# One decoder step on one core: merge statistics in one group, gate rows early, another order of delta heads, five early gate tiles

## The chip, the cores and the metric

The kernel runs on one core of a Trainium2 chip. The metric is the device time of one execution in microseconds (us); three runs of the kernel before took 942.03, 938.55 and 942.79 us, median 942.03 us. Engines are named as the profile names them: PE is TensorE (matmul), PEld its weight load, DVE is VectorE, ACT is ScalarE, POOL is GpSimd, SP is SyncE, which issues nearly all DMAs here and does no arithmetic.

## The reference

One layer of a hybrid decoder, in float32, for one prompt of 512 tokens and 8 samples of 4 new tokens each (544 token columns), model width 1024. Cut to what matters:

```python
shift, scale, gate = split(silu(c) @ w_cond + b_cond, 3)
h = x * (1 + scale) + shift
qa, ka, va, za, qkv_b, zb, a_b, b_b, ga, gb = split_columns(h @ w_in)       # 11280 columns
# branch A: 3 groups of 8 heads, windows 128/512/2048 with dilation 1/4/16
for g in range(3): out[g], lse[g] = dilated_attend(qa[g], ka[g], va[g], bias[g])
o_a = einsum('g..., g...d -> ...d', softmax(lse over g), out)               # the merge
ya = o_a * silu(za)
# branch B: 8 delta heads: causal conv (width 4) + silu, l2norm, chunked delta rule
state, o_b = gated_delta(state0, q, k, v, g, beta)
yb = rmsnorm(o_b) * b_norm_w * silu(zb)
merged = sigmoid(ga) * (ya @ w_branch_a) + sigmoid(gb) * (yb @ w_branch_b)
y = layernorm(ALPHA * x + gate * (merged @ w_out)) * ln_g + ln_b
```

The samples also read caches of keys and values and states of the delta rule; caches and states are outputs too.

## The kernel before, in words

**The stream.** The projection `h @ w_in` is cut into 88 column tiles of 128 columns. One tile is one job: its weight is loaded by SP (512 KB), split into a high and a low part (`hi` by ACT, `lo` by DVE), and multiplied in 2 halves of 272 token columns, 8 pieces of the contraction and 3 products each, so 48 matmuls of 128x272 (`pp<-hhi,hi`, `pp<-hlo,hi`, `pp<-hhi,lo`). A half lies in one of two PSUM banks (`pp`) until ACT and DVE have read it out (`evac`); only then can the half after the next begin. Jobs run strictly in the order of the list `jobs`.

**The order before.** With c0 to c7 for the three jobs (k, q, v) of a delta head (`conv_job`) and r0 to r3 for the nine jobs of an attention round (two heads of each of three groups, `attention_job`), the list is c0, r0, c1, c2, r1, c3, c4, r2, c5, c6, six jobs of r3, c7, three jobs of r3, za0, za1, zb0, zb1, za2, za3, zb2 to zb7, then gate and branch jobs.

**Beside the stream** run threads of other work, planned with lower rank numbers (0 first): the delta rule (`delta_rule`, rank 0), its preparation (`delta_blocks`, rank 1), prompt attention (`prompt_attention`, rank 3), attention of the samples over their caches for the first half of the heads (`early`, rank 4); the stream has rank 9. A planner in the kernel (`Recorder.schedule`) lists all instructions with costs and dependences and writes each engine's order; the hardware then runs each engine's list in order, with semaphores. Operations inside `with rec.together():` are held together: once the first is taken, PE takes nothing else until the last.

**Buffers the change touches.** A head's k and q lie in a tile `KQ`, of which there are two. So the first conv of head h+2 (`KQ<-ext,acc` on DVE) can write only after the last matmul of head h's delta rule that reads it (`pd<-S,KQ`). Conv rows `ext` have two buffers as well. Pool `op` (tag `o`) has nine buffers of 128x544 for slabs of early sample attention, later for `zt`, `nd`, `ybh` and `yal`, handed out in the order of first use.

**The merge.** After rounds 1 and 3 the minima and sums of the softmax (`st`) are turned by 40 small matmuls into `pt` (`pg<-cst,st`), DVE and ACT make weights `R`, these go to DRAM and come back broadcast (`dw<-R`, `wv<-dw`), and DVE weighs `ya` and `NB`. The matmuls of one strip of 32 PE columns (one value of r) follow one another, then the next strip's; they are not held together.

**The boundary after round 3.** The jobs zb0 and zb1 are early (`EARLY_B = 2`): their `zt` lies in pool `op` and they are finished later. The `zt` of zb2 to zb7 lies in a pool `zp` that opens only when the pools of attention and delta rule are closed, so after the last merge operation. Behind the boundary lies the samples' chain: `sample_decays` (tile `nd`), `sample_delta`, and sample attention of the second half of the heads (`kv` tiles), whose result is copied into `ya`; the branch jobs of A (`pp<-yah,hi`) need it. Seven gate jobs of A (`EARLY_A = 7`) stand ahead of them.

**The gate rows** (`gate_rows`, rank 1, the last stretch of the stream): `gate` of prompt and samples, `silu(c) @ w_cond[:, 2048:]`, in 16 matmuls with 32 columns of weights (`pd<-wc,cs`), then four selecting matmuls (`pg<-Y,cst`: for each half one that repeats the prompt's row 128 times into `gp` and one that spreads the samples' rows into `gs`), added to the bias.

Of the kernel before, what the change touches and what calls it, by code (L numbers as in the profile page):

```python
# [11 lines left out]
F32 = mybir.dt.float32  # L12
# [23 lines left out]
BANKS = (2, 2, 3, 1)  # L36
MOVE = 128
MOVES = (48.0, 850.0)
EARLY_A, EARLY_B = 7, 2
S0B = 7  # L40


# [201 lines left out]
class Recorder:  # L244
# [20 lines left out]
    def pool(self, make, name, bufs, side):  # L265
        return Pool(self, make, name, bufs, side)
# [456 lines left out]
def body(ctx, tc, io):  # L723
# [71 lines left out]
    def cond_product(part, load, ps):  # L795


        for k, n, wc in load(part):
            q = (k + 2 * n) % 4
            pe.matmul(ps[n][32 * q:32 * q + 32, :], cs[:, k, :], wc, start=(k < 4), stop=(k >= 4),  # L800
                      tile_position=(0, 32 * q))
            yield

    def cond_rows(part, k0, nk):
        return io["w_cond"][k0 * 128:(k0 + nk) * 128, part * D:(part + 1) * D].rearrange("(k p) c -> p k c", p=128)
# [165 lines left out]
    tail = d0.tile([128, 34], F32, name="tail")  # L971
    etot = d0.tile([128, 34], F32, name="etot")
    dO = dram.tile([8, 128, 512], F32, name="dO")
    qd = dram.tile([2, 2, NS, 256], F32, name="qd")
    us = d0.tile([128, 3, 8, NS], F32, name="us")
    oS = keep.tile([128, 8, NS], F32, name="oS")
# [406 lines left out]
    def attention_job(j, g, s):  # L1383

        def begin():
            pairs[j][s, g] = spare()[:, :SEQ] if s == 2 else ap.tile([128, 512], F32, name="qk"[s], bufs=3)

        def evac(n, ps):
            t, scale = pairs[j][s, g], 1.0 if s else -0.125
            if g == 0:  # L1390
                lo, hi = ((0, 272), (272, 512))[n]
                se.activation(t[:, lo:hi], ps[:, 0:hi - lo], AF.Copy, scale=scale)
            else:
                v = t.rearrange("p (r a n) -> p n a r", r=4, a=4)
                m = (17, 15)[n]
                se.activation(v[:, 17 * n:17 * n + m], ps[:, 0:16 * m].rearrange("p (n a r) -> p n a r", a=4, r=4),
                              AF.Copy, scale=scale)
            if n:
                se.activation((qs, ks, vs)[s][:, j, g, :], ps[:, 240:272], AF.Copy, scale=scale)
                if s == 2:  # L1400
                    threads.set(ready[j, g], 2.5)

        return column_job(("a", j, g, s), evac=evac, begin=begin, start=(freed[j - 1] if j else began,))

    def prompt_attention():

        for j in range(4):
# [95 lines left out]

            pt = pg()
            ve.memset(pt, 1.0)
            for kd in range(4):
                for r in range(4):
                    o = pt[32 * r:32 * r + 4, 128 * kd:128 * kd + 128]
                    if kd % 2:
                        pe.matmul(o, st[:, kd, r, :], ident, start=True, stop=True, tile_position=(0, 32 * r))  # L1510
                        continue
                    for i in range(4):
                        pe.matmul(o.rearrange("p (a n) -> p n a", a=4)[:, 8 * i:8 * i + 8, :], st[:, kd, i, :],
                                  ident[:, r:128:4], start=True, stop=True, tile_position=(0, 32 * r))
            R = ap.tile([128, 4, 128], F32, name="R", tag="P", bufs=2)
            Z = ap.tile([128, 4, 128], F32, name="Z", tag="P", bufs=2)
            two = lambda t: t[:, None, :].to_broadcast([128, 2, 128])
# [437 lines left out]

    def gate_rows():

        b = io["b_cond"][:, 2 * D:]
        sp.dma_start(gp, b.to_broadcast([128, D]))
        sp.dma_start(gs, b.to_broadcast([64, D]))  # L1960
        ps = [pd(), pd()]
        yield 4.0
        for n in range(2):
            w = slice(512 * n, 512 * n + 512)

            for k0 in range(0, KT, 4):
                wc = []
                for k in (k0, k0 + 2):
                    wc.append(wcp.tile([128, 2, 512], F32, name="wc"))
                    sp.dma_start(wc[-1], cond_rows(2, k, 2)[:, :, w])  # L1970
                with rec.together():
                    take(cond_product(2, lambda part: ((k0 + k, n, wc[k // 2][:, k % 2]) for k in range(4)), ps), 99)
                yield 2.0
            Y = zp.tile([128, 512], F32, name="Y", tag="rbo")
            se.activation(Y, ps[n], AF.Copy)
            yield 1.8
            for t, r, sel in ((gp, 128, C("selc")[:, 0:1].to_broadcast([128, 128])), (gs, 64, C("selg"))):
                p = pg()
                pe.matmul(p[0:r], sel, Y, start=True, stop=True)
                ve.tensor_add(t[:, w], t[:, w], p[0:r])  # L1980


    for s in (1, 0, 2):
        jobs.append(conv_job(0, s))
    h = 1
    for j in range(4):
        nine = [attention_job(j, g, s) for g in range(3) for s in range(3)]
        if j == 3:
            jobs += nine[:6] + [conv_job(7, s) for s in (1, 0, 2)] + nine[6:]
        else:  # L1990
            jobs += nine + [conv_job(h + i, s) for i in range(2) for s in (1, 0, 2)]
            h += 2
    jobs += [za_job(j) for j in range(2)] + [zb_job(h, True) for h in range(EARLY_B)] + [za_job(j) for j in range(2, 4)]
    jobs += [zb_job(h) for h in range(EARLY_B, 8)]
    mt, yah, yal, mhi, mlo = {}, {}, {}, {}, {}
    mT = mt
    of_b = (lambda k: ybh[k], lambda k: ybl[k])
# [19 lines left out]
    def early():  # L2017
# [4 lines left out]
        yield tuple(ready[3, g] for g in range(3))  # L2022
        sample_queries(1, slabs()[0:64, 0:256], qr1)

    threads.add(early(), 4)

    def prep():
# [62 lines left out]
            se.activation(wo[n][0][:, k:k + 2], raw, AF.Copy)  # L2090
            ve.tensor_sub(wo[n][1][:, k:k + 2], raw, wo[n][0][:, k:k + 2].bitcast(F32))

    wctx = ExitStack()
    wcp = pool(wctx, "wcp", 3, "right")

    def merge_after(m):
        def after():
            t = gate_tile["ga", m]
# [10 lines left out]

    for m in range(8):  # L2110
        jobs += [gate_job("ga", m)] * (m >= EARLY_A) + [branch_job("ga", m, 4, of_a, after=merge_after(m))]
    threads.add(gate_rows(), 1)
    threads.add(stream(len(jobs)), 9)
    threads.run(lambda: not threads.parts)
    wctx.close()
    zctx.close()
    gates_ctx.close()
    octx.close()
# [181 lines left out]
```

## Time and profile before

| | us |
|---|---|
| median of three runs | 942.03 |
| profiled execution | 939.77 |
| its span | 938.0 |
| PE busy | 892.0 |
| DVE busy | 736.8 |
| ACT busy | 417.0 |

The profile is of one execution; 1.8 us of its time lie outside the span. A busy PE is not a PE at its peak, since matmuls overlap: the stream's matmuls start 0.125 us apart while each is recorded as 0.29 us long. A program's matmul in plain float32 appears as two records. In a row of the timeline stand start, duration, engine, line (L670 is the planner's helper, so instructions are told apart by their tiles), operation, out<-in, shape and, in square brackets, how long the engine sat idle before and what ended it. In a row of windows stand the stretch, its length, then busy time and number of instructions of each engine, the granted PE clock, the busy share of the 16 DMA engines and GB/s.

### The profile page before, as it was taken

To read this page: it belongs to the slowest core of one execution; us is meant where nothing else is said; L and a number is where in the kernel's file an instruction comes from. 1 tells how busy PE (TensorE), PEld (TensorE's weight loads), DVE (VectorE), ACT (ScalarE), POOL (GpSimd) and SP (SyncE) were. 2 spreads that over 40 slices of the span, in tenths; PEclk is the share of its full clock that TensorE was granted. 3 is DMA by queue.
4 is the path that set the end of the run, shared out by engine and by line. 5 is a ranking of instruction groups with operands and counts; after the bars stand their busy time and mean duration, and the time that the engine had idled before them with its cause. 6 is when DMAs were issued, how large, how long until landed. Compare 5 with 4: busy or idle time off the path is not lost.

```text
span 938.0 us, 20669 instructions
## 1 busy us (share of the span) xinstructions
PE 892.0 (95%) x8070; PEld 825.8 (88%) x8070; DVE 736.8 (79%) x1620; ACT 417.0 (44%) x975; POOL 64.0 (7%) x176
## 2 busy tenths in 40 slices
PE   4799999999999999999999998988999999999995
PEld 1599999999989999979999997877999999998784
DVE  1575556876799999889989997556899789957768
ACT  0365347753557443576725753441532222234411
POOL 0120000200011110010100200001020000000000
PEclk9799999999999999999999999998999999999998
DMA  9677773658878778786787868459689899988613
GB/s 357 226 220 238 221 246 136 224 182 251 272 249 273 229 250 287 236 292 219 241 301 242 277 206 298 140 172 365 219 267 360 340 418 377 361 284 306 205 43 112
DMA packets 106341, 237.76 MB, mean 253 GB/s; under 512 B 30898, under 2 KB 62140, under 8 KB 103556
## 3 DMA queue, kind: packets, MB, share of 16 engines
q1 hardware_dynamic: 106244, 236.45, 73.8%
q8 instruction: 63, 1.03, 0.4%
q14 instruction: 34, 0.28, 0.1%
HBM read 220.40 MB, written 103.70 MB: 346 GB/s over the span
## 4 chain that ended last, share of the span: by engine, by line
PE 72%; DVE 11%; DMA 4%; ACT 3%; issue 2%; SPq 0%; POOL 0%; DVEq 0%; POOLq 0%; ACTq 0%
PE pp L670 55%; PE pg L670 7%; PE pd L670 6%; PE pb L670 3%; DVE slab L670 2%; DMA dO<-orow 1%; DMA wv<-dw 1%; DMA slab<-in_vs 1%; DVE lo L670 1%; ACT L670 1%; DVE XF L670 1%; DVE r L670 1%; ACT hi L670 1%; DVE ya L670 1%; DVE acc L670 0%
## 5 line engine op out<-in xcount | busy, mean ns | idle before, releaser
L670 PE MATMUL pp<-hhi,hi 128*128 128x272 f32 x1408 | 415.6, 295 | 11.3 <-DVE zt L670 8.7
L670 PE MATMUL pp<-hhi,lo 128*128 128x272 f32 x1408 | 415.3, 295 | 0.0
L670 PE MATMUL pp<-hlo,hi 128*128 128x272 f32 x1408 | 414.1, 294 | 0.2 <-DVE small L670 0.2
L670 PEld LDWEIGHTS pp<-hhi,hi 128*128 128x128 f32 x1408 | 267.2, 190 | 13.7 <-DVE zt L670 9.1
L670 PEld LDWEIGHTS pp<-hlo,hi 128*128 128x128 f32 x1408 | 267.2, 190 | 2.7 <-issue 0.9
L670 PEld LDWEIGHTS pp<-hhi,lo 128*128 128x128 f32 x1408 | 266.5, 189 | 3.3 <-issue 1.8
L670 ACT ACTIVATE hi<-wt 128x1024 fp32r<-128x1024 f32 (+1 forms) x104 | 106.8, 1027 | 167.7 <-PE pp L670 144.8
L670 DVE TENSOR_TENSOR lo<-wt,hi 128x1024 fp32r<-128x1024 f32 (+1 forms) x104 | 122.5, 1178 | 54.8 <-ACT hi L670 54.0
L670 DVE SCALAR_TENSOR_TENSOR acc<-ext,cw,acc 128x568 f32<-128x568 f32 x72 | 57.5, 799 | 0.7
L670 ACT ACT_TABLE_LOAD x38 | 48.8, 1283 | 9.3 <-DMA cT<-in_cT 8.0
L670 DVE TENSOR_TENSOR slab<-slab 128x512 f32<-128x512 f32 (+1 forms) x66 | 42.4, 663 | 3.7 <-DMA slab<-in_vs 3.1
L670 DVE TENSOR_REDUCE slab<-slab 128x8 f32<-128x512 f32 (+2 forms) x66 | 42.4, 655 | 0.3
L670 ACT ACTIVATE P<-P,st 128x256 f32<-128x256 f32 (+1 forms) x64 | 31.3, 491 | 19.7 <-DVE st L670 19.5
L670 PE MATMUL pp<-ybl,hi 128*128 128x272 f32 x128 | 37.0, 289 | 0.0
L670 PE MATMUL pp<-ybh,lo 128*128 128x272 f32 x128 | 37.0, 289 | 0.0
L670 PE MATMUL pp<-ybh,hi 128*128 128x272 f32 x128 | 36.8, 288 | 0.0
L670 ACT ACTIVATE zt<-pp 128x272 f32<-128x272 f32 x48 | 18.4, 389 | 34.7 <-PE pp L670 31.7
L670 POOL COPY cx<-ext 128x3 f32<-128x3 f32 (+1 forms) x48 | 23.3, 515 | 94.0 <-ACT ext L670 93.9
L670 ACT ACTIVATE vn<-pd,beta 128x128 f32<-128x128 f32 x32 | 11.7, 366 | 34.4 <-PE pd L670 34.3
L670 DVE TENSOR_TENSOR Tb<-Tb,tmp 32x15 f32<-32x15 f32 (+7 forms) x120 | 23.4, 195 | 4.1
L670 PE MATMUL pp<-wc,cs 128*32 128x512 f32 x64 | 13.1, 916 | 14.3 <-DMA wc<-in_w_cond 14.3
L670 ACT ACTIVATE ext<-pp 128x272 f32<-128x272 f32 (+2 forms) x72 | 20.0, 314 | 14.9 <-PE pp L670 13.9
(395 smaller groups left out, 1574.3 us busy)
## 6 DMA issues: line engine op xcount, KB each, us to landing
out_kv_s<-in_cache SPq DMA_DIRECT2D x144, 512.0 KB
wt<-in_w_in SPq DMA_DIRECT2D x88, 512.0 KB
out_kv_s<-in_cache SPq DMA_DIRECT2D x24, 496.0 KB
wc<-in_w_cond SPq DMA_DIRECT2D x8, 1024.0 KB
slab<-in_ks SPq DMA_DIRECT2D x32, 256.0 KB
slab<-in_vs SPq DMA_DIRECT2D x32, 256.0 KB
kv<-in_ks SPq DMA_DIRECT2D x16, 512.0 KB
kv<-in_vs SPq DMA_DIRECT2D x16, 512.0 KB
```

Source lines behind the costliest of these rows:

```text
L670: getattr(real[x.engine], x.name)(*map(arg, x.args), **{k: arg(v) for k, v in x.kw.items()})
```

## The change

- **Merge statistics**: the 40 small matmuls of a merge run inside one `together`, and four successive ones now go to four different strips.
- **Gate rows**: made right after the first gates, in a thread of rank 5, with tiles of pool `op`. Each half loads eight pieces of 256 KB, multiplies them in one group, needs one selecting matmul (73 rows: those of the nine conditions, the prompt's first, and 64 with the samples' rows spread over their tokens) instead of two, and writes to a DRAM tile `dg`. Where `gate_rows` stood, two DMAs read `dg` into `gp` and `gs`.
- **Order**: c0, r0, c1, r1, c2, c3, r2, c4, c5, three jobs of r3, c6, three of r3, c7, three of r3, za0 and so on as before.
- **Early tiles**: `EARLY_B` is 5: zb2, zb3 and zb4 put `zt` into pool `op` and stand ahead of the boundary.

```diff
-EARLY_A, EARLY_B = 7, 2
+EARLY_A, EARLY_B = 7, 5
...
+    dg = dram.tile([73, D], F32, name="dg")
...
-            for kd in range(4):
-                for r in range(4):
-                    o = pt[32 * r:32 * r + 4, 128 * kd:128 * kd + 128]
-                    if kd % 2:
-                        pe.matmul(o, st[:, kd, r, :], ident, start=True, stop=True, tile_position=(0, 32 * r))
-                        continue
-                    for i in range(4):
-                        pe.matmul(o.rearrange("p (a n) -> p n a", a=4)[:, 8 * i:8 * i + 8, :], st[:, kd, i, :],
-                                  ident[:, r:128:4], start=True, stop=True, tile_position=(0, 32 * r))
+            with rec.together():
+                for kd, i in ((kd, i) for kd in range(4) for i in range(1 if kd % 2 else 4)):
+                    for r in range(4):
+                        o = pt[32 * r:32 * r + 4, 128 * kd:128 * kd + 128]
+                        if kd % 2:
+                            pe.matmul(o, st[:, kd, r, :], ident, start=True, stop=True, tile_position=(0, 32 * r))
+                        else:
+                            pe.matmul(o.rearrange("p (a n) -> p n a", a=4)[:, 8 * i:8 * i + 8, :], st[:, kd, i, :],
+                                      ident[:, r:128:4], start=True, stop=True, tile_position=(0, 32 * r))
...
     def gate_rows():
...
+        sel = cst[:, CCOLS["selc"][0]:CCOLS["selc"][0] + 73]
         for n in range(2):
             w = slice(512 * n, 512 * n + 512)
+            wc = [op.tile([128, NT], F32, name="wg", tag="o")[:, 0:512] for _ in range(KT)]
+            for k in range(KT):
+                sp.dma_start(wc[k], io["w_cond"][128 * k:128 * k + 128, 2 * D + 512 * n:2 * D + 512 * n + 512])
+            ps = {n: pd()}
+            yield 6.0
+            with rec.together():
+                take(cond_product(2, lambda part: ((k, n, wc[k]) for k in range(KT)), ps), 99)
+            Y = op.tile([128, NT], F32, name="Y", tag="o")[:, 0:512]
             se.activation(Y, ps[n], AF.Copy)
+            rows = op.tile([128, NT], F32, name="grow", tag="o")[0:73, 0:512]
+            sp.dma_start(rows, io["b_cond"][:, 2 * D + 512 * n:2 * D + 512 * n + 512].to_broadcast([73, 512]))
+            yield 3.0
+            p = pd()
+            pe.matmul(p[0:73], sel, Y, start=True, stop=True)
+            ve.tensor_add(rows, rows, p[0:73])
+            sp.dma_start(dg[:, w], rows)
+            yield 1.0
...
+    nine = [[attention_job(j, g, s) for g in range(3) for s in range(3)] for j in range(4)]
+    conv = [[conv_job(h, s) for s in (1, 0, 2)] for h in range(1, 8)]
+    jobs += nine[0] + conv[0] + nine[1] + conv[1] + conv[2] + nine[2] + conv[3] + conv[4] + nine[3][:3] + conv[5] + nine[3][3:6] + conv[6] + nine[3][6:]
+    jobs += [za_job(j) for j in range(2)] + [zb_job(h, True) for h in range(2)] + [za_job(j) for j in range(2, 4)]
+    jobs += [zb_job(h, h < EARLY_B) for h in range(2, 8)]
...
+    threads.add(gate_rows(), 5)
     threads.add(early(), 4)
...
-    threads.add(gate_rows(), 1)
+    sp.dma_start(gp, dg[0:1].to_broadcast([128, D]))
+    sp.dma_start(gs, dg[9:73])
     threads.add(stream(len(jobs)), 9)
```

More of the change, by code (lines that the diff above doesn't have):

```diff
@@ L1956, in gate_rows @@
     def gate_rows():
[L1958 to L1962, printed above, removed]
+        sel = cst[:, CCOLS["selc"][0]:CCOLS["selc"][0] + 73]
         for n in range(2):
             w = slice(512 * n, 512 * n + 512)
[L1966 to L1974, printed above, removed]
-            se.activation(Y, ps[n], AF.Copy)
[L1976 to L1980, printed above, removed]
+            wc = [op.tile([128, NT], F32, name="wg", tag="o")[:, 0:512] for _ in range(KT)]
[6 more added lines that the diff above has]
+            Y = op.tile([128, NT], F32, name="Y", tag="o")[:, 0:512]
+            se.activation(Y, ps[n], AF.Copy)
+            rows = op.tile([128, NT], F32, name="grow", tag="o")[0:73, 0:512]
[6 more added lines that the diff above has]
+            yield 1.0
@@ L1983, in body @@
     for s in (1, 0, 2):
         jobs.append(conv_job(0, s))
[L1985 to L1993, printed above, removed]
@@ L1994, in body @@
-    jobs += [zb_job(h) for h in range(EARLY_B, 8)]
+    nine = [[attention_job(j, g, s) for g in range(3) for s in range(3)] for j in range(4)]
[3 more added lines that the diff above has]
+    jobs += [zb_job(h, h < EARLY_B) for h in range(2, 8)]
@@ L2091, in load_out @@
             ve.tensor_sub(wo[n][1][:, k:k + 2], raw, wo[n][0][:, k:k + 2].bitcast(F32))
-    wctx = ExitStack()
-    wcp = pool(wctx, "wcp", 3, "right")
     def merge_after(m):
@@ L2111, in body @@
         jobs += [gate_job("ga", m)] * (m >= EARLY_A) + [branch_job("ga", m, 4, of_a, after=merge_after(m))]
-    threads.add(gate_rows(), 1)
+    sp.dma_start(gp, dg[0:1].to_broadcast([128, D]))
+    sp.dma_start(gs, dg[9:73])
     threads.add(stream(len(jobs)), 9)
     threads.run(lambda: not threads.parts)
-    wctx.close()
     zctx.close()
```

## The prediction

> **What bounds the kernel now.** I read the page's first rows, then PE's waits, windows around the longest wait, and the timeline there. PE is busy 95% of the span. Of the idle rest, the start (the loads of `wc`) and the tail are not touched; in the middle stands one long wait.
>
> ```profile
> PE 892.0 (95%) x8070; PEld 825.8 (88%) x8070; DVE 736.8 (79%) x1620; ACT 417.0 (44%) x975; POOL 64.0 (7%) x176
> PE pp L670 <- DMA wc<-in_w_cond: 14.3, 6, 10.6
> PE pp L670 <- DVE zt L670: 9.2, 2, 8.7
> 620.00:640.00 20.00, 11.06 (x74) 10.38 (x74) 12.94 (x22) 5.29 (x8) 3.50 (x8) 0.77 0.82 265
> ```
>
> The timeline shows it at the boundary after round 3. Both PSUM banks of the stream hold zb2, whose read-out into `zt` is listed on DVE behind the merge, because its pool opens only after it. Behind the wait PE is slow: matmuls 0.22 us apart, where 0.125 us is usual.
>
> ```profile
> 630.54 1.02 DVE L670 TENSOR_TENSOR ya<-ya,wv 128x512 f32<-128x512 f32 x1 [0.48 <-DMA wv<-dw]
> 636.35 0.69 DVE L670 SCALAR_TENSOR_TENSOR ya<-ya,spare 128x512 f32<-128x512 f32 x1
> 636.96 0.78 DVE L670 SCALAR_TENSOR_TENSOR zt<-zt,pp 128x272 f32<-128x272 f32 x2
> 637.44 0.59 PE L670 MATMUL pp<-hhi,hi 128*128 128x272 f32 x1 [8.75 <-DVE zt L670]
> 637.84 0.43 PE L670 MATMUL pp<-hlo,hi 128*128 128x272 f32 x1
> 638.06 0.43 PE L670 MATMUL pp<-hhi,lo 128*128 128x272 f32 x1
> ```
>
> A busy PE does not yet mean that saved PE time shortens the end. Two chains run beside it. One is the samples' chain from the boundary to the branch jobs of A:
>
> ```profile
> 829.32 0.44 DVE L670 COPY ya<-os__7978 128x32 f32<-128x32 f32 x4
> 835.39 0.73 DVE L670 TENSOR_TENSOR yal<-ya,yah 128x544 fp32r<-128x544 f32 x1 [0.72 <-ACT yah L670]
> 835.50 0.29 PE L670 MATMUL pp<-yah,hi 128*128 128x272 f32 x1
> 692.00:822.00 130.00, 130.00 (x1079) 128.55 (x1078) 120.66 (x145) 34.25 (x64) 2.63 (x3) 1.00 0.99 368
> 835.48:874.60 39.12, 39.12 (x282) 31.98 (x280) 29.32 (x52) 17.24 (x31) 0.00 (x0) 1.00 0.73 259
> ```
>
> The last `yal` is made while PE starts the first branch: stream and samples arrive together, without slack on either side. From 692 to 822 DVE is busy 120.66 of 130 us, the DMA engines 0.99, so this chain can't be pressed together; it moves with the boundary.
>
> The other is the chain of delta heads through the two `KQ` tiles. Before, c6 met its limit just so: the write of `KQ` starts when the last read by head 4 has ended (439.39 + 0.39 = 439.78).
>
> ```profile
> 439.39 0.39 PE L670 MATMUL pd<-S,KQ 128*128 128x128 f32 x2
> 439.82 0.69 DVE L670 SCALAR_TENSOR_TENSOR KQ<-ext,acc 128x512 f32<-128x512 f32 x1
> 123.75:253.80 130.05, 105.38 (x725) 94.28 (x723) 0.00 (x0) 15.40 (x46) 1.00 0.66 209
> 252.55:394.45 141.90, 109.35 (x764) 98.83 (x763) 0.00 (x0) 16.27 (x48) 1.00 0.78 261
> 385.00:511.70 126.70, 95.55 (x648) 84.44 (x648) 0.00 (x0) 12.79 (x41) 1.00 0.75 251
> 498.75:618.85 120.10, 83.45 (x560) 73.15 (x559) 4.69 (x11) 11.09 (x31) 0.99 0.66 223
> ```
>
> These four windows (PE counts only the stream's `pp` matmuls, 48 a job) run from the first matmul of c1, c3, c5 and c7 to the last read of that head's `KQ`: a head keeps its tile 120 to 142 us after its first conv matmul.
>
> **The change, part by part.** All against the profiled execution, 939.77 us; the median, 942.03, is 2.3 us above it.
>
> *Merge statistics.* The first merge's 80 records run in one piece, the second's in six, between matmuls of the delta rule.
>
> ```profile
> 306.38 2.65 PE L670 MATMUL pg<-cst,st 128*4 128x32 f32 x80
> 604.29 1.08 PE L670 MATMUL pg<-cst,st 128*4 128x32 f32 x28
> 606.48 0.28 PE L670 MATMUL pg<-cst,st 128*4 128x32 f32 x2
> 607.85 0.28 PE L670 MATMUL pg<-cst,st 128*4 128x32 f32 x2
> 609.17 0.38 PE L670 MATMUL pg<-cst,st 128*4 128x128 f32 x2
> 610.40 0.67 PE L670 MATMUL pg<-cst,st 128*4 128x128 f32 x14
> 612.18 1.31 PE L670 MATMUL pg<-cst,st 128*4 128x32 f32 x32
> 614.88 0.69 DVE L670 COPY R<-pg 128x512 f32<-128x512 f32 x1
> L670 PE MATMUL pg<-ks,Qz 128*32 128x32 f32 x96 | 1.9, 199 | 0.0
> L670 PE MATMUL pb<-S,KP 128*32 128x128 f32 x128 | 4.5, 275 | 0.0
> ```
>
> The last two rows already go round the four strips: 1.9/96 = 0.020 us a record at 32 columns, 4.5/128 = 0.035 at 128. So 64 x 0.020 + 16 x 0.035 = 1.8 us a merge: 2.65 - 1.8 = 0.8 saved in the first, 4.0 - 1.8 = 2.2 in the second. What counts more: the second's end moves from 613.49 to 604.29 + 1.8 = 606.1, and `R`, `dw`, `wv` and the merge behind it come 7.4 us sooner. PE holds for it what is queued behind, at most 1.8 us of head 7's rule. [...]
>
> *Gate rows.* Leaving the last stretch: 4.3 + 2.1 + 2.0 = 8.4 us of PE, 2 x 1.4 us of DVE, and the loads.
>
> ```profile
> L670 PE MATMUL pd<-wc,cs 128*32 128x512 f32 x32 | 4.3, 605 | 0.0
> L670 PE MATMUL pg<-Y,cst 128*64 128x512 f32 x4 | 2.1, 618 | 0.0
> L670 PE MATMUL pg<-Y,cst 128*128 128x512 f32 x4 | 2.0, 592 | 0.0
> L670 DVE TENSOR_TENSOR gp<-gp,pg 128x512 f32<-128x512 f32 x2 | 1.4, 688 | 1.9 <-PE pg L670 1.9
> L670 DVE TENSOR_TENSOR gs<-gs,pg 64x512 f32<-64x512 f32 x2 | 1.4, 680 | 0.8 <-PE pg L670 0.8
> L670 DVE TENSOR_TENSOR wo0l<-wo,wo0h 128x1024 fp32r<-128x1024 f32 x4 | 4.8, 1216 | 2.7 <-ACT wo0h L670 2.7
> ```
>
> There PE has 39.12 of 39.12 us and DVE 29.32, so PE's loss shows: at most 8.4 us, at least 0 if the split of `w_out` sets the end. I take 8.4 - 2.7 = 5.7, since the wait for `wo0h` stays. Added early: 4.3 + 2.0 = 6.3 us of PE, in a stretch where PE is dense, so all on the path. Sixteen loads of 256 KB, two of the bias and two stores pass SP's queue ahead of cache moves and beside the stream's weights, which are three buffers ahead; I cost them at nothing; without that cover PE waits, for at most the 10.6 us that it waited for such loads at the start. The group holds PE until all eight pieces are there, with the stream behind it: part of the same bound. The two reads of `dg` in the tail replace two reads of the bias: nothing.
>
> *Order.* c4 now starts after r2, and c6 only nine jobs later, where before it was fifteen. Head 4 will free its `KQ` some 127 to 142 us after c4's start, like the heads that follow a round. The stream can do c4, c5, three jobs of r3 and c6, 12 jobs or 576 matmuls; then c6's third conv has no `ext`, both banks are full, and in-order PE stands. In the three windows after rounds the stream did 725, 764 and 648 matmuls: 149, 188 and 72 too many. At 0.125 us that is 18.6, 23.5 and 9 us, and some 2.5 us until a bank is free again (the `KQ` write, 0.69, and a read-out of 0.4). So the new wait is 11.5 to 26 us, nothing at the low end if the head is quicker. The nearest row is c5's (also after r2), the other two are higher; I take 16, and 1.4 us for slow matmuls behind it (14 x 0.1, as behind the wait of today). Other heads keep 12 or 15 jobs between them, as before, and cost nothing; if c7 too waits, it is within c6's delay.
>
> *Early tiles.* zb2, zb3 and zb4, 18 us of PE, stand where PE waited. The 8.75 us and the 1.4 of slow matmuls go. Late next: `nd`, which now gets its buffer only after zb4's `zt`; it delays `sample_decays` by 5 us, but the first state loads end later, so nothing (bounds 0 and 5).
>
> *The sum*, in the order of time:
>
> 1. Before round 3 ends: +6.3 - 0.8 + 17.4 = +22.9. One other wait, 3.1 us of PE for `st`, may vanish with sample attention earlier; I take half: +21.4.
> 2. The merge ends at +21.4 - 7.4 = +14.0, and the samples' chain starts there. DVE owes the stream about one job less behind the boundary (a split of 1.2 us and two read-outs of 0.4): +12.0.
> 3. The stream itself: +21.4 - 2.2 - 8.75 - 1.4 = +9. The later of both counts: +12.0.
> 4. The tail: +12.0 - 5.7 = +6.3, so 946 us for an execution like the profiled one, and with the 2.3 us between it and the median 948.
>
> **The rivals.** *The heads keep up (ends on the other side).* If head 4 is freed before PE runs out of 12 jobs, the 17.4 us are not there: merge +21.4 - 17.4 - 7.4 = -3.4, samples -5.4, with the tail -11.1: 929 us, 931 as a median. It decides at about 12 us less for a head than c5's 126.7. For it: c7's 120.1, with DVE less loaded. Against: no head was quicker, and c6 met the limit with fifteen jobs between. *The early loads are late.* PE stands in a group for up to 10.6 us: 948 + 10.6 = 959. Against: the DMA engines have spare time in that stretch; for: sixteen loads at once. *A short wait.* If it is 5 us instead of 17.4, the chain of the samples allows +12.0 - 12.4 - 5.7 = -6.1: 936 as a median, a milder form of the first. *Nothing moves*: waits and gains cancel, 940 to 944.
>
> **How the numbers follow.** All as medians. A wait at c6 of 11.5 to 26 us gives 943 to 958, itself the likeliest case's range: chance 0.52. Heads that keep up, wholly or nearly (929 to 937): 0.32. Late loads on top: 0.09. Cancelled: 0.07. A difference under 0.5% (4.7 us) is about what can't be told from no change. The first case is slower in 0.42 and the same in 0.10 (its lower fifth); the second is faster; the third slower; the last is the same in 0.05 and faster in 0.02. So faster 0.34, same 0.15, slower 0.51. The range 928 to 961 takes in both ends.
>
> **What will show it.** In windows of the stream, a PE wait of over 10 us behind c6's third conv, ended by ACT's or DVE's work on `ext` or `KQ` (right), or none (the first rival). The second merge's statistics in one piece of about 1.8 us. No wait of 8.75 us at the merge. No `wc` records in the last stretch, and it shorter by 5 to 6 us. The first `pp<-yah,hi` about 12 us later than 835.50. The prediction is wrong if PE passes c6 without a stop, or if the end moves without the samples' chain.

## The result, and the profile after

The changed kernel takes 956.41 us (median; 955.71 to 958.4), the kernel before beside it on the same chip 941.17 us. The ratio is 1.0168, with a 95% interval of 1.015 to 1.0186: slower by 1.7%, some 15 us, where the forecast had 6. The profiled execution took 955.71 us with a span of 953.9. The first rows of its page:

```profile
span 953.9 us, 20655 instructions
PE 901.8 (95%) x8066; PEld 833.7 (87%) x8066; DVE 733.1 (77%) x1618; ACT 412.1 (43%) x973; POOL 66.8 (7%) x176
```

PE has four instructions less than before and is busy 9.8 us longer. Where the time went is seen in a windows view over the same three stretches of work in both kernels: from the first matmul of attention round 0 to the first of c1, from the first matmul of c5 to that of the job nine later (its 52nd), and from the first matmul on `yah` to the end. Columns: from and to in us, the length, then busy time (and instructions) of PE, PEld, DVE, ACT and POOL, the granted clock, the DMA engines' share, GB/s. First the kernel before:

```profile
63.80:123.80 60.00, 59.86 (x473) 59.15 (x472) 30.92 (x77) 28.89 (x64) 3.23 (x9) 1.00 0.74 233
385.10:472.90 87.80, 86.51 (x861) 80.57 (x860) 80.57 (x218) 59.33 (x163) 11.01 (x33) 1.00 0.74 247
835.50:938.00 102.50, 91.74 (x554) 74.81 (x552) 76.43 (x138) 31.01 (x53) 0.00 (x0) 0.97 0.49 168
```

and the changed one:

```profile
64.00:146.80 82.80, 73.95 (x573) 66.35 (x572) 34.23 (x86) 29.87 (x66) 4.27 (x11) 0.92 0.66 214
401.30:499.10 97.80, 91.62 (x906) 84.76 (x904) 91.77 (x248) 55.56 (x147) 12.46 (x32) 0.97 0.71 244
857.30:953.90 96.60, 85.36 (x512) 74.68 (x512) 75.25 (x136) 30.87 (x52) 0.00 (x0) 0.95 0.44 150
```

The first stretch is 22.8 us longer: 14.1 of busy PE and 8.7 idle, at a granted clock of 0.92 where it was 1.00. The second, with c6 in it, is 10.0 us longer. The last is 5.9 us shorter. DVE's waits in the first stretch of the changed kernel (total us, times, longest) show the place:

```profile
DVE grow L670 <- DMA grow<-in_b_cond: 8.6, 2, 4.7
```

and so does its timeline around the two loads of the bias (start, us, engine, and in brackets the idle time ahead and what ended it):

```profile
65.08 0.42 SPq L670 DMA_DIRECT2D grow<-in_b_cond  x1
...
75.20 0.68 DVE L670 TENSOR_TENSOR grow<-grow,pd 73x512 f32<-73x512 f32 x1 [3.92 <-DMA grow<-in_b_cond]
...
90.95 0.28 SPq L670 DMA_DIRECT2D grow<-in_b_cond  x1
...
101.36 0.68 DVE L670 TENSOR_TENSOR grow<-grow,pd 73x512 f32<-73x512 f32 x1 [4.66 <-DMA grow<-in_b_cond]
...
104.94 1.65 PE L670 MATMUL pb<-KQ 128*128 128x256 f32 x3 [4.34 <-DVE QKd L670]
```

A load of 146 KB takes 10 us from issue to use, both times; DVE stands in order before it, and PE behind DVE. What such a load does to the DMA engines is seen where it is alone, in a stretch with no other traffic (windows view of the changed kernel):

```profile
98.30:100.00 1.70, 1.70 (x16) 1.70 (x15) 0.00 (x0) 0.88 (x1) 0.00 (x0) 1.00 0.06 24
```

The share of 0.06 is that of one engine of sixteen (1/16 = 0.0625). In the same 1.7 us the trace has 20 packets, one row of 2 KB each 0.08 us: the packets of all 73 rows go one after the other, from 94.85 to 100.85, 6 us. The trace doesn't name a packet's engine; that it is one and the same throughout is the author's reading of this share and this order. The two stores `dg<-grow` have 73 rows too and go the same way: the packets of the second run singly from 103.56 to 110.46.

The statistics run in one piece, and the first matmul on `yah` comes 21.8 us later than before, still waiting for ACT's `yah`, which the samples' chain feeds (timeline):

```profile
624.34 1.58 PE L670 MATMUL pg<-cst,st 128*4 128x32 f32 x80
...
857.31 0.51 PE L670 MATMUL pp<-yah,hi 128*128 128x272 f32 x2 [2.09 <-ACT yah L670]
```

### The profile page after: what moved, and what is told of

Same layout as the page of the kernel before. It is cut to its first block, busy times and chain, and to the rows that moved or that the text cites. A ratio compares the mean times of both kernels' runs of the same rounds, so it can differ in the third digit from the quotient of the medians.

```text
span 953.9 us, 20655 instructions
## 1 busy us (share of the span) xinstructions
PE 901.8 (95%) x8066; PEld 833.7 (87%) x8066; DVE 733.1 (77%) x1618; ACT 412.1 (43%) x973; POOL 66.8 (7%) x176
## 4 chain that ended last, share of the span: by engine, by line
PE 75%; DVE 12%; DMA 8%; ACT 3%; issue 2%; SPq 1%; DVEq 0%; ACTq 0%
PE pp L670 58%; PE pg L670 7%; PE pd L670 6%; PE pb L670 3%; DVE lo L670 2%; DVE acc L670 2%; DVE slab L670 1%; DMA wc<-in_w_cond 1%; DMA wg<-in_w_cond 1%; DMA grow<-in_b_cond 1%; DMA dr<-rrow 1%; SPq L670 1%; ACT L670 1%; DVE r L670 1%; DVE NTs L670 1%
## 5 line engine op out<-in xcount | busy, mean ns | idle before, releaser
L670 POOL COPY cx<-ext 128x3 f32<-128x3 f32 (+1 forms) x48 | 25.6, 562 | 92.8 <-ACT ext L670 92.8
L670 ACT ACTIVATE spare<-pp 128x272 f32<-128x272 f32 (+1 forms) x32 | 16.1, 503 | 27.6 <-PE pp L670 27.6
L670 DVE TENSOR_TENSOR tmp<-Ls,Tb 32x15 f32<-32x15 f32 (+7 forms) x120 | 23.1, 192 | 3.9 <-DMA Ls<-dblk 0.5
```

What stands on the lines that cost most here:

```text
L670: getattr(real[x.engine], x.name)(*map(arg, x.args), **{k: arg(v) for k, v in x.kw.items()})
```

## The experiments

The table is worked out from each kernel's timeline. "Early" is the first stretch above (round 0's first matmul to c1's), "c5 + 9" the second (in e10 other jobs: c5 and six of r3). The other columns are points of time in us: the end of the last read of `KQ` (head 7 is then over), the merge's last write to `ya`, the last write to `nd`, the issue of the first store of a delta state of the samples, the first matmul on `yah`. "Tail" is from there to the end of the span. The runs stand in the order of their labels. The medians come from four sessions, and the kernel before, run in each, took 941.2 to 942.3 us, so differences between rows of different sessions are uncertain by about 1 us; each ratio is to the kernel before of its own session. The points of time are of one profiled execution each.

| kernel | median us | early | c5 + 9 | last KQ | ya | nd | state store | yah | tail |
|---|---|---|---|---|---|---|---|---|---|
| before | 941.2 to 942.3 | 60.0 | 87.8 | 618.9 | 637.0 | 639.0 | 687.3 | 835.5 | 102.5 |
| changed | 956.41 | 82.8 | 97.8 | 655.4 | 653.6 | 682.2 | 715.8 | 857.3 | 96.6 |
| e1 gate rows alone | 947.51 | 82.6 | 85.2 | 636.2 | 646.5 | 648.5 | 699.7 | 847.9 | 98.3 |
| e2 order alone | 950.68 | 59.8 | 97.4 | 645.2 | 634.7 | 650.1 | 700.8 | 848.9 | 101.3 |
| e3 statistics + tiles | 951.12 | 59.9 | 86.1 | 625.2 | 630.1 | 660.3 | 697.0 | 837.8 | 112.2 |
| e4 changed, 80 rows | 944.27 | 68.4 | 98.1 | 644.4 | 642.6 | 670.7 | 704.1 | 845.6 | 96.6 |
| e5 e4 + nd early | 947.02 | 68.2 | 97.3 | 640.4 | 638.7 | 649.3 | 702.4 | 843.6 | 97.4 |
| e6 e4, old order | 936.83 | 68.3 | 84.2 | 623.2 | 629.9 | 665.2 | 699.7 | 836.2 | 98.3 |
| e7 e6 + nd early | 927.71 | 67.4 | 84.1 | 623.0 | 629.1 | 631.9 | 682.6 | 831.2 | 93.3 |
| e8 e3 + nd early | 935.03 | 59.9 | 84.9 | 621.4 | 626.8 | 629.9 | 684.1 | 825.6 | 106.2 |
| e9 changed, bias sooner | 954.32 | 77.5 | 97.9 | 655.6 | 653.9 | 682.8 | 716.8 | 858.2 | 96.7 |
| e10 e5, c6 later | 945.15 | 68.2 | 88.5 | 643.7 | 644.4 | 653.9 | 708.4 | 845.1 | 98.1 |
| e11 statistics alone | 944.78 | 59.9 | 86.1 | 623.6 | 628.1 | 631.4 | 687.4 | 828.0 | 114.4 |
| e12 tiles alone | 944.72 | 59.9 | 86.9 | 618.9 | 637.8 | 660.8 | 697.0 | 832.9 | 111.6 |

The order of all engines is planned anew for each kernel, so a part taken alone is its edit together with what the planner then makes of the rest. I began with theory A (the early gate rows cost most of what was not forecast) against theory C (the new order does).

**e1, the gate rows alone.** The kernel before with the new `gate_rows`, its thread, `dg` and the two reads of it.

```diff
...
+    threads.add(gate_rows(), 5)
     threads.add(early(), 4)
...
-    threads.add(gate_rows(), 1)
+    sp.dma_start(gp, dg[0:1].to_broadcast([128, D]))
+    sp.dma_start(gs, dg[9:73])
```

> The kernel before with one part of the change: the gate rows worked out early, stored to dg, and read back for the tail; order, merge statistics and early tiles as before. Theory A (the early gate rows carry most of the loss, some 17 us more than the 6.3 forecast): first matmul of c1 near 146 instead of 123.8, and, less the 5.7 to 5.9 us that the tail gains, 12 to 18 us slower, 953 to 959. Theory C (the new place of c6 carries the loss, the early rows cost what was forecast): +6.3 - 5.7, so 940 to 944, and c1 not later than 131.

947.51 us, ratio 1.0058 (1.0037 to 1.0079), between the two theories. The early stretch is that of the changed kernel, 82.6 us. So the loss there belongs to the gate rows and to nothing else in the change. But the end is not as late: of the 22.6 us lost, nearly half is given back by the first matmul on `yah` (12.4 later than before), and 4.2 more in the tail.

**e2, the order alone.**

```diff
...
-        if j == 3:
-            jobs += nine[:6] + [conv_job(7, s) for s in (1, 0, 2)] + nine[6:]
-        else:
-            jobs += nine + [conv_job(h + i, s) for i in range(2) for s in (1, 0, 2)]
...
+    jobs += nine[0] + conv[0] + nine[1] + conv[1] + conv[2] + nine[2] + conv[3] + conv[4] + nine[3][:3] + conv[5] + nine[3][3:6] + conv[6] + nine[3][6:]
```

> The kernel before with the new order of conv jobs and rounds alone (one head between rounds 0 and 1). Theory A: only the wait at c6, about 10 us as read from the jobs of the changed kernel (401.3 to 499.1 against 385.1 to 472.9), so 8 to 12 us slower, 949 to 953. Theory C: the whole loss and the gains given away, 18 us slower or more, 959 and over. By the forecast's own term, 17.4 us, 958.

950.68 us, ratio 1.0091 (1.006 to 1.0122), as theory A has it. c5 + 9 is 9.6 us longer. The stream itself stands longer at c6, from 466.94 to 483.76, but PE is busy with other work for 10.3 of these 16.8 us. What no theory had is the last read of `KQ`: head 7 ends at 645.2 instead of 618.9, after the merge (634.7), where before it ended 18 us ahead of it. The samples' chain follows head 7: the merge ends 2.3 us sooner than before and `nd` is loaded early (600.27), but the first loads of the states are issued 2.1 us behind head 7's store `dO`, and the first state store comes 13.5 us later than before (timeline of e2):

```profile
648.51 0.33 SPq L670 DMA_DIRECT2D dO<-orow  x1
...
650.57 1.69 SPq L670 DMA_DIRECT2D S<-in_state_delta  x2
```

**e3, statistics in one piece and five early tiles.**

```diff
-EARLY_A, EARLY_B = 7, 2
+EARLY_A, EARLY_B = 7, 5
...
-            for kd in range(4):
-                for r in range(4):
+            with rec.together():
+                for kd, i in ((kd, i) for kd in range(4) for i in range(1 if kd % 2 else 4)):
+                    for r in range(4):
...
```

> The kernel before with the merge statistics in one piece and five early branch-B tiles, without the early gate rows and with the old order. All theories: second merge's statistics in one piece of 1.6 to 1.8 us, no 8.7 us wait at the boundary, the samples' chain some 7 us sooner, so 6 to 10 us faster, 931 to 935. If the samples' chain does not decide there, but the stream, 8.75 + 1.4 + 2.2 = up to 12 us faster, 929.

951.12 us, ratio 1.0094 (1.0062 to 1.0126): slower, where every theory had it faster. The merge does end 6.9 us sooner, and the stream runs ahead by up to 19 us, but `nd` is ready at 660.3 instead of 639.0, the samples' chain starts 9.7 us late, and the tail is 10 us longer. e5, e7, e8 and e12 go after `nd`, e11 and e12 after the tail.

**e4, eighty rows.** The changed kernel with the bias tile and `dg` seven rows higher, and the selecting matmul and the addition with them; the seven rows of `dg` are never read. So the two loads and the two stores all change from 73 rows to 80.

```diff
-    dg = dram.tile([73, D], F32, name="dg")
+    dg = dram.tile([80, D], F32, name="dg")
...
-            rows = op.tile([128, NT], F32, name="grow", tag="o")[0:73, 0:512]
-            sp.dma_start(rows, io["b_cond"][:, 2 * D + 512 * n:2 * D + 512 * n + 512].to_broadcast([73, 512]))
+            rows = op.tile([128, NT], F32, name="grow", tag="o")[0:80, 0:512]
+            sp.dma_start(rows, io["b_cond"][:, 2 * D + 512 * n:2 * D + 512 * n + 512].to_broadcast([80, 512]))
...
```

> The changed kernel with the bias tile and dg of 80 rows instead of 73 (the seven more are never read). Theory A (the bias load of 73 rows goes row by row through one DMA engine, a 2 KB packet each 0.08 us, and DVE and SP stand behind it): the load lands 2 to 3 us after its issue instead of 10, DVE's waits for it (8.6 us) go, c1 starts at 128 to 138 instead of 146.8, and the time is 6 to 17 us under the changed kernel's 956.4: 939 to 950. Theory B (the sixteen loads of w_cond pass SP's queue ahead of the stream's weights and PE is held in the groups, whatever the bias does): 953 to 957, c1 within 3 us of 146.8.

944.27 us, ratio 1.0018 (1.0002 to 1.0034): 12.1 us of the changed kernel's 15 are gone. Its windows over the first stretch and over a piece of it in which the second bias load lands:

```profile
65.10:133.50 68.40, 67.04 (x573) 61.46 (x572) 34.23 (x86) 29.81 (x66) 4.28 (x11) 1.00 0.81 259
...
87.50:89.00 1.50, 1.50 (x15) 1.50 (x13) 0.00 (x0) 0.27 (x1) 0.00 (x0) 1.00 1.04 341
```

and DVE's waits there:

```profile
DVE grow L670 <- DMA grow<-in_b_cond: 1.3, 1, 1.3
```

The engines stand in almost the same order as in the changed kernel, and the number of PE instructions is the same, 573. PE's busy time falls from 73.95 to 67.04 (the clock is 1.00 again) and its idle time from 8.9 to 1.4. Seven unneeded rows make the load faster: its 80 packets take 2.6 us (87.53 to 90.17), up to nine at a time, where 73 took 6.0 one by one, and with the other loads the DMA engines are all busy (1.04). The share of 0.06 fits one engine for 73 rows; for 80 the trace shows many packets at a time, but other loads share the engines, so how many the load got can't be counted. That 80 rows would load faster than 73 had no run behind it when it was expected; the runs show that they do, not why. From issue to landing the second load still takes 6.0 us (84.13 to 90.17), not the 2 to 3 expected.

**e9, the 73 rows sooner** (told here as it belongs to e4). The load is issued ahead of the eight of `w_cond`, so that DVE need not wait for it. The stores stay as they are, with 73 rows.

```diff
+            rows = op.tile([128, NT], F32, name="grow", tag="o")[0:73, 0:512]
+            sp.dma_start(rows, io["b_cond"][:, 2 * D + 512 * n:2 * D + 512 * n + 512].to_broadcast([73, 512]))
             wc = [op.tile([128, NT], F32, name="wg", tag="o")[:, 0:512] for _ in range(KT)]
...
             se.activation(Y, ps[n], AF.Copy)
-            rows = op.tile([128, NT], F32, name="grow", tag="o")[0:73, 0:512]
-            sp.dma_start(rows, io["b_cond"][:, 2 * D + 512 * n:2 * D + 512 * n + 512].to_broadcast([73, 512]))
```

> The changed kernel, still with 73 rows, but each bias load issued ahead of its eight loads of w_cond, so that it has landed long before DVE's addition. Theory A1 (the price of the bias loads is DVE's wait in order, 8.6 us, with what stands behind it): the wait goes, c1 starts at 133 to 140 instead of 146.8, time 943 to 950. Theory A2 (the price is that one DMA engine is held for 6 us and the share of every later load that is on that engine comes late, whenever DVE needs the rows): c1 within 4 us of 146.8, 952 to 957.

954.32 us, ratio 1.0131 (1.0111 to 1.0152): A2. DVE no longer waits for the rows, but now for other loads (DVE's waits of e9, first stretch); `cr` was issued 0.85 us behind a load of the rows, `rb` 27 us behind it:

```profile
DVE NTs L670 <- DMA cr<-drows: 5.5, 1, 5.5
...
DVE QKd L670 <- DMA rb<-dr: 2.5, 1, 2.5
```

Of the 14.4 us between the early stretches of the changed kernel and e4, e9 wins back 5.3; 9.1 stay. So DVE's wait in order is the smaller part. The rest fits A2, which supposes that the engine of the rows carries a share of other loads too; how much of it the two 73-row stores cost, which e4 widens and e9 leaves, was not tried apart. In the changed kernel's trace 256 packets of 4 KB start between 66.44 and 78, as many as the two loads of 512 KB issued there have, the weights at 66.44 and `bias` at 67.37. Of these, 240 start by 73.76; eight start one after the other from 74.38 to 75.60, and eight more from 76.42 to 77.53. Eight is one sixteenth of a load's 128. The trace doesn't tell whose a packet is; that these are one engine's share of each load, late behind the rows, is the author's estimate from the counts and the page's 16 engines.

**e5, e6, e7: `nd` and the order, on top of eighty rows.** For `nd`, the tile is allocated and loaded by the early samples' thread, ahead of zb2 in the program, and no longer in `sample_decays`; for e6 the order is that of before (the diff of e2, taken back); e7 has both.

```diff
+    def load_decays():
+        nd = two_tiles(op.tile([128, NT], F32, name="nd", tag="o"))
+        for G in range(2):
+            sp.dma_start(nd[:, 1, G, :], drows2[G:G + 1, :].to_broadcast([128, 128]))
+        return nd
...
         sample_queries(1, slabs()[0:64, 0:256], qr1)
+        decays.append(load_decays())
...
-        yield from sample_decays(op.tile([128, NT], F32, name="nd", tag="o"))
+        yield from sample_decays(decays[0])
...
```

> The changed kernel with 80 rows, and nd allocated and loaded at the end of the early samples' thread, ahead of zb2 to zb4 in the program, so that it no longer gets its buffer behind zb4's zt. Theory N (the late nd holds the samples' chain back: with 80 rows alone nd was ready at 670.65, 28 us after the merge's last write to ya at 642.64, where the kernel before has 2 us): nd's products within 3 us of the merge, the first store of a delta state at 692 to 699 instead of 704.08, the first matmul on yah at 836 to 842 instead of 845.56, time 935 to 941. Rival M (the loads of the states and the stream hold the chain as much as nd did): the first matmul on yah within 2 us of 845.6, time 942 to 946.

> The changed kernel with 80 rows and the job order of before (two heads between rounds 0 and 1). If the order costs here what it cost alone (8.4 us as a median): 934 to 938, job 51 without the 10 us lost since job 42. If what the order costs is hidden by the late nd or by the loads: 941 to 945.

> Both: 80 rows, the order of before, and nd loaded early. Theory N and the order's cost together: 944.3 - 8.4 - (4 to 8) = 928 to 932, under both kernels. Rival M: no better than with the order of before alone, 934 to 938.

e5: 947.02 us, ratio 1.0056 (1.0031 to 1.0081), no gain; theory N missed, and rival M's 942 to 946 as well, by 1 us. (e5's ten times lie from 941.3 to 950.0, and the profiled one took 942.75, so its median against e4's settles only that there is no gain of N's size.) e6: 936.83 us, ratio 0.9948 (0.993 to 0.9966), as expected if the order passes its cost on. e7: 927.71 us, ratio 0.9857 (0.9832 to 0.9882), 1.4% under the kernel before and the fastest of all. The timelines, first e6, in which `nd` is loaded after zb4 and is ready 35 us after the merge:

```profile
651.15 0.91 SPq L670 DMA_DIRECT2D nd<-drows  x2
...
664.78 0.41 DVE L670 TENSOR_TENSOR nd<-nd,cd 128x256 f32<-128x256 f32 x1
...
699.66 0.41 SPq L670 DMA_DIRECT2D out_delta_s<-S  x1
```

then e7, in which it is loaded at 592 and the states follow the merge at once:

```profile
591.74 0.82 SPq L670 DMA_DIRECT2D nd<-drows  x2
...
628.45 0.69 DVE L670 SCALAR_TENSOR_TENSOR ya<-ya,spare 128x512 f32<-128x512 f32 x1
...
631.48 0.41 DVE L670 TENSOR_TENSOR nd<-nd,cd 128x256 f32<-128x256 f32 x1
...
682.62 0.40 SPq L670 DMA_DIRECT2D out_delta_s<-S  x1
```

and e5, in which `nd` is early too, but head 7 is not over:

```profile
640.06 0.39 PE L670 MATMUL pd<-S,KQ 128*128 128x128 f32 x2
...
643.49 0.33 SPq L670 DMA_DIRECT2D dO<-orow  x1
...
646.26 1.01 SPq L670 DMA_DIRECT2D S<-in_state_delta  x2
```

The samples' chain goes on when three things are there: the merge, head 7's end (the states' loads follow its store `dO`, in e5 by 2.8 us, as in e2), and `nd`. The table shows where `nd` decides: in the changed kernel, e3, e4, e6, e9 and e12 the first state store comes 33 to 37 us after `nd`, in the others 48 to 56 us after it. In the changed kernel the last two are late together. Taking the late `nd` away alone shows no gain, since head 7 then holds the chain; taking the order away alone shows 7.4 us, and `nd` then binds; both together give 16.6 us (944.27 to 927.71). The order moves the merge too (642.6 in e4, 629.9 in e6), so its 7.4 us are not head 7's alone.

**e8, statistics and tiles with `nd` early**: e3 with the same edit.

> The kernel before with merge statistics in one piece and five early tiles, and nd loaded early. Theory N (alone, the two parts made it slower, 951.1, since nd waited for zb4's zt and was ready 30 us after the merge): the samples' chain goes with the merge, the first store of a delta state at 680 to 688 instead of 696.95, the first matmul on yah at 828 to 833, the gate rows' loads in the tail sooner with it, time 931 to 938. Rival M: the state loads hold the chain, and the time stays at 946 to 952.

935.03 us, ratio 0.9946 (0.9927 to 0.9965), as theory N has it: 16.1 us under e3 for one tile allocated sooner. Against e7, whose further difference is the early gate rows with eighty rows, it is 7.3 us slower: the gate rows, loaded well, are worth that much.

**e10, c6 three jobs later.**

```diff
... (the end of the line `jobs +=`)
-nine[3][:3] + conv[5] + nine[3][3:6] + conv[6] + nine[3][6:]
+nine[3][:6] + conv[5] + conv[6] + nine[3][6:]
```

> 80 rows, nd loaded early, and the new order, but c6 after six jobs of round 3 instead of three, so twelve jobs after c4's start instead of nine. Theory K (the order costs what the wait for head 4's KQ at c6 costs, and head 7 ends later by it): from c5's first job to c7's first some 114 us, as before (113.7), instead of 122; the last read of KQ at 628 to 634 instead of 640; time 930 to 938. Rival L (what costs is that one head instead of two stands between rounds 0 and 1, so that every head from the third on is late): no gain, 941 to 948, last read of KQ at 638 or later.

945.15 us, ratio 1.004 (1.0025 to 1.0055): no gain, as rival L has it. The wait at c6 is gone, and PE stands at c7 instead, until head 5's last read of `KQ`. Windows from c5's first matmul to c7's, and on to za0's, of e5:

```profile
389.40:510.50 121.10, 115.15 (x1144) 107.21 (x1143) 113.81 (x300) 67.61 (x181) 14.69 (x43) 0.96 0.73 244
510.50:559.40 48.90, 48.79 (x433) 46.72 (x432) 46.11 (x108) 27.58 (x69) 3.90 (x12) 1.00 0.76 246
```

and of e10:

```profile
390.20:500.00 109.80, 108.66 (x1063) 103.04 (x1062) 104.09 (x274) 64.90 (x169) 12.65 (x35) 1.00 0.77 251
500.00:559.80 59.80, 55.41 (x501) 50.51 (x500) 54.56 (x135) 34.60 (x83) 7.67 (x18) 0.94 0.75 247
```

In e10's timeline the stream, which stopped at 525.1, goes on 1.2 us after that read:

```profile
534.35 0.39 PE L670 MATMUL pd<-S,KQ 128*128 128x128 f32 x2
...
535.95 0.40 PE L670 MATMUL pp<-hhi,hi 128*128 128x272 f32 x1 [1.21 <-ACT ext L670]
```

170.0 us for both stretches in e5, 169.6 in e10. The wait is moved, not removed. Whether the two `KQ` tiles or the rules, which run head by head, set this pace was not tried (a third tile of 4 KB a partition would tell), and stays open.

**e11 and e12, statistics alone and tiles alone.** Each has one half of e3: e11 the grouped loop, e12 the tiles.

```diff
-EARLY_A, EARLY_B = 7, 2
+EARLY_A, EARLY_B = 7, 5
...
-    jobs += [zb_job(h) for h in range(EARLY_B, 8)]
+    jobs += [zb_job(h, h < EARLY_B) for h in range(2, 8)]
```

> The kernel before with the merge statistics in one piece alone. By the forecast's term (second merge's statistics end 7.4 us sooner, the samples' chain with them): ya's last write at 629 to 631 instead of 637, nd with it, 934 to 937. If the group that holds PE costs head 7 as much as the merge gains: 940 to 944. If the group itself is what made statistics and tiles together slower: 946 to 952.

> The kernel before with five early branch-B tiles alone. Theory N: nd gets its buffer behind zb4's zt and is loaded near 645 instead of 582.9, its products at 655 or later, the first store of a delta state at 697 or later, time 948 to 955. By the forecast (nd late costs nothing; the 8.75 us wait goes, but the samples' chain decides): 938 to 942.

e11: 944.78 us, ratio 1.0037 (1.0018 to 1.0056). e12: 944.72 us, ratio 1.0029 (1.0 to 1.0059). Neither is where it was expected. In e12 `nd` is as late as theory N has it (660.8), but the time is 3 us better than its range: the first matmul on `yah` comes 2.6 us sooner than before, and what is lost is lost in the tail, 9.1 us longer. In e11 the first matmul on `yah` comes 7.5 us sooner, the forecast's 7.4, and the tail then takes 114.4 us instead of 102.5. Its timeline, where the old gate rows still stand, shows why:

```profile
876.70 1.07 PE L670 MATMUL pd<-wc,cs 128*32 128x512 f32 x8
...
881.78 2.36 DVE L670 TENSOR_TENSOR wo1l<-wo,wo1h 128x1024 fp32r<-128x1024 f32 x2 [10.84 <-ACT wo1h L670]
...
886.72 0.77 PE L670 MATMUL pp<-wo0h,mhi 128*128 128x512 f32 x1 [6.11 <-DVE lo L670]
```

and ACT's wait from 860 to 900:

```profile
ACT Y L670 <- PE pd L670: 8.2, 1, 8.2
```

The last product of the gate rows stands behind 9 us of products of `w_out` on PE (867.3 to 876.7), ACT waits for it in order, the second half of `w_out` is split late, and PE stops. In the kernel before that product stood ahead of those of `w_out`, at 867.44. In e3 and e12 it stands behind them as in e11, and PE stops at the same place for 3.7 us. With the gate rows out of the tail (e7) the tail is 93.3 us. So the gain of the statistics is lost where the planner puts the gate rows late. They need not leave the tail for it: in e8 they stand there too, all ahead of `w_out` (the last product at 861.9, `w_out` from 868.7), and the kernel is 0.5% under the one before.

## Why the prediction was wrong

The direction was right, the size was not: +15 us for +6. Counted along the forecast's own path, in the profiled executions, the merge ended 2.6 us later than forecast and the first matmul on `yah` 9.8 us later: most of the miss arises between the two, in step 2. The gate rows cost more than that, but in the count up to the merge other errors covered them.

*Step 1, the gate rows: failed.* "I cost them at nothing" was said of the sixteen loads, the two of the bias and the two stores, with 10.6 us as the bound. So the early stretch was to grow by PE's 6.3 us; it grew by 22.8 with 73 rows and by 8.4 with 80. The term was bounded by the loads of `wc`, which are 128 rows high; the loads of the bias and the stores have 73, and no DMA of the kernel before had that shape. The sixteen loads of `w_cond`, the ones that the rival "the early loads are late" had in mind, cost less: PE waited 1.8 us for `wg`, and 3.35 us at a granted clock of 0.50 followed. The 73 rows alone are the 12.1 us by which e4 is faster. That e4, at 944.27 us, lies 4 us from the forecast's 948 is in part luck, since the term for c6 was too large and the lateness of head 7 and `nd` left out.

*Step 1, c6: mechanism right, term too large.* The wait is there, ended as foreseen when head 4 frees its `KQ` (timeline of the changed kernel):

```profile
488.64 0.29 PE L670 MATMUL pp<-hhi,lo 128*128 128x272 f32 x1
...
497.29 0.64 PE L670 MATMUL pd<-S,KQ 128*128 128x128 f32 x2
...
497.96 0.69 DVE L670 SCALAR_TENSOR_TENSOR KQ<-ext,acc 128x512 f32<-128x512 f32 x1 [0.66 <-PE pd L670]
...
499.14 0.59 PE L670 MATMUL pp<-hhi,hi 128*128 128x272 f32 x1 [1.21 <-ACT ext L670]
```

The stream stands for 10.2 us, and PE, which works on the delta rule meanwhile, for 5.6 of them. In c5 + 9 it costs 10.0 us, where 17.4 stood in the sum. Head 4 kept its `KQ` for 123.9 us, less than the 127 to 142 assumed, and 1.2 us passed from its last read to the stream's next matmul, where 2.5 were put. The nearest row that the forecast had, c5's 9.0 us, would have given 10.2 with these 1.2; it took 16 from between its three rows, and 1.4 more. By its own sum a term of 10.0 gives some 941 us, no change: that the result lies inside its 943 to 958 is luck. Between c1 and c5 6.8 us of what was lost early came back, where 2.3 stood in the sum (0.8 of statistics, 1.5 of the wait for `st`). The count at the end of round 3 came out near the forecast, +24.8 for +21.4, as the errors had different signs; that is luck too.

*Step 2, the samples' chain: failed.* The statistics are right: one piece of 1.58 us for the 1.8 forecast, and the merge ended 16.6 us later than before, for +14.0. But "the samples' chain starts there" was wrong: 12.0 us were put for the chain, and 21.8 came at `yah`. The first state store came 28.5 us later than before, as the chain waited also for `nd` (682.2 for 639.0) and for head 7 (655.4 for 618.9). Head 7's end stands in no term; the nearest words are "if c7 too waits, it is within c6's delay". `nd` was seen and priced at nothing: "it delays `sample_decays` by 5 us, but the first state loads end later, so nothing (bounds 0 and 5)". In the changed kernel it is loaded at 665 (583 in the kernel before), and its delay behind the merge went from 2 to 28.6 us:

```profile
665.21 0.90 SPq L670 DMA_DIRECT2D nd<-drows  x2
...
681.80 0.41 DVE L670 TENSOR_TENSOR nd<-nd,cd 128x256 f32<-128x256 f32 x1
```

That head 7 alone can hold the chain is seen in e2, that `nd` can in e6 against e7 (9.1 us); with the old order and an early `nd` together 16.6 us are won (e4 to e7). On the way to `yah` 6.7 us of the 28.5 were made up.

*Step 3: right.* The stream is not what decides; PE waits 2.09 us for ACT's `yah`.

*Step 4: right.* 5.7 us forecast, 5.9 measured, no `wc` in the last stretch.

*The early tiles*: the wait of 8.75 us on `zt` is gone, as forecast, but the stream's lead is worth nothing where the samples' chain binds. Their price is `nd`, 16.1 us beside the statistics (e3 to e8). Alone they make the kernel no faster (e12), and there the loss lies in the tail.

*The rivals.* "The heads keep up" fell: all kernels with the new order lost some 10 us at c6, or in e10 at c7. "The early loads are late" named the right place and a price (959) close to the result, but not the right loads; it had 0.09. "A short wait" was half true: 10.0 us came, between its 5 and the forecast's 17.4.

## What to carry to other kernels

A load is priced by its own shape: look for a row of that shape, and if there is none, bound it by one engine's pace, here 24 GB/s, not by that of a load of another shape, and count what may come late beside it: with DVE's wait for the rows gone, 9.1 of the 14.4 us stayed (e9). A chain that starts when several things are there gains only what the latest allows, so when one of them moves, write down the times of the others; here that would have shown head 7 and `nd`. And where two waits cover each other, undo both at once before calling either free.

## What the runs showed of the hardware

A DMA of 73 rows moved 24 GB/s (one 2 KB packet each 0.08 us, share 0.06, 6.0 us for all), one of 80 rows was done in 2.6 us with up to nine packets at a time and other loads beside it (share 1.04), and behind the first load of 73 rows the last 16 of 256 packets of 4 KB, a size that the rows' packets don't have, started one after the other from 74.38 to 77.53, the other 240 by 73.76. In the kernel's time seven more rows in two loads and two stores gained 12.1 us. In that stretch PE's 573 instructions took 73.95 us of busy time instead of 67.04, at a granted clock of 0.92 for 1.00: nearly half of the 14.4 us is PE running slower, not PE standing. The three waits of PE there, by its waits:

```profile
PE pb L670 <- DVE QKd L670: 4.3, 1, 4.3
PE pb L670 <- DVE rc L670: 2.7, 1, 2.7
PE pd L670 <- DMA wg<-in_w_cond: 1.8, 1, 1.8
```

and windows in each wait, in order of time, with the one behind it:

```profile
73.70:76.30 2.60, 0.00 (x0) 0.00 (x0) 1.07 (x6) 0.00 (x0) 0.00 (x0) 1.00 0.94 311
76.85:80.20 3.35, 3.35 (x15) 3.07 (x13) 1.53 (x6) 2.03 (x4) 0.00 (x0) 0.50 0.64 223
87.40:89.10 1.70, 0.00 (x0) 0.00 (x0) 0.31 (x1) 0.00 (x0) 0.00 (x0) 1.00 0.29 122
90.50:93.85 3.35, 3.35 (x12) 2.23 (x11) 0.00 (x0) 0.32 (x1) 0.00 (x0) 0.50 0.59 184
100.70:104.10 3.40, 0.00 (x0) 0.00 (x0) 2.74 (x6) 0.00 (x0) 0.00 (x0) 1.00 0.49 160
104.15:110.90 6.75, 5.96 (x23) 5.49 (x24) 4.19 (x10) 0.48 (x1) 0.00 (x0) 0.50 0.60 182
```

In the second window of each pair the granted clock is 0.50 throughout, 3.35, 3.35 and 6.75 us; the last starts 0.8 us before PE goes on. PE is busy for 12.66 us of them. That is worth some 6.3 us, an estimate from half of these 12.66, and so most of the 6.9 us of busy time. In e4, where PE's longest wait of the stretch is 1.0 us, the clock stays at 1.00. So in this stretch half clock came with waits of 4.3, 2.7 and 1.8 us, and in e4 not with one of 1.0 us. How short a wait can be was not tried.
